# A scan planned in a fixed round of products: one change to a bidirectional RWKV-7 layer on Trainium2

## Chip, cores and metric

The kernel runs on one core of one Trainium2 chip. The metric is the device time of one execution in microseconds (us). Lower is better. The core has a matrix engine (TensorE, PE in the profile; its weight loads are PEld), a vector engine (VectorE, DVE), an activation engine (ScalarE, ACT), a general engine (GpSimd, POOL), a queue engine that issues transfers (SyncE, SP) and 16 DMA engines.

## The reference

One layer over 128 context tokens and 2048 latent tokens of width 1024. Tokens are normalised and modulated, one projection gives eight parts, half of the width goes through a bidirectional RWKV-7 scan (8 heads of 64), the other half through a gated short convolution, and a second projection with a residual and a last normalisation makes the output.

```python
h = _rmsnorm(x, lp['norm_g']) * (1.0 + scale) + shift
proj = h @ lp['w_in']
...
def step(S, inp):
    r_t, w_t, k_t, v_t, kk_t, a_t = inp
    s_kk = jnp.einsum('bdhij,bdhj->bdhi', S, kk_t)
    S = (S * w_t[..., None, :] - s_kk[..., :, None] * (kk_t * a_t)[..., None, :]
         + v_t[..., :, None] * k_t[..., None, :])
    return S, jnp.einsum('bdhij,bdhj->bdhi', S, r_t)
...
yb = b_gate * _short_conv(c_gate * u_conv, lp['conv_w'], is_latent) * jax.nn.silu(g_b)
u = jnp.concatenate([ya, yb], axis=-1) @ lp['w_out']
return x + gate * u, s_final
```

All inputs and outputs are float32.

## The kernel before

The work has three phases. **Phase 1** (`phase1`, from L56) goes over three pairs of token blocks and makes all projections. For each pair, `turn(h, ga, gb)` does a half of group `ga` of the scan's inputs (`mixA`, `gateA`) and, beside it, a half of group `gb` of the convolution (`partB`: `convB` or `gateB`). In the last pair, two convolution groups run in the turns and groups 2 and 3 behind them, in a loop that advances `K.early()`: this generator issues the products F and G of the scan's stages 0 and 1, and their inverses.

**Phase 2** (`phase2`, from L780) is the scan in chunks of 64 tokens. There are 17 stages: 4 head pairs x 4 token blocks of 512, and one for the context. A stage has eight chunks in each direction. For each stage:

- `matrices(s)` (L1078): the products F and G on PE from `rr` (L935), masked from PSUM to SBUF by DVE (L938). The blocks on the diagonal of G are put together by ACT and DVE into `dg` (L947, L950), stored, and loaded as `ab` (`load_ab`).
- `inverse(s)`: `invert` on POOL, L963 to L979, 54 instructions that invert these blocks into `zt`, and a store of `zt` on POOL's own queue. The plan has it as one operation of 24.5 us.
- `blocks(s)` (L1107): loads `zt` back as `zc`, transposes it on DVE to `zr` (L1112), and makes U (L997) and W (L1002) on PE, with copies by ACT.
- `operands` and `merge`: loads, queries Q (transposes, L1022), product X (L1009), and the eight operator products E (L1017), which DVE masks into `E` (L1165).
- `steps(s, i)`: the step of each direction, on PE (L1185). It reads `sv`, and DVE scales its sum by the decay into the next `sv` (L1206): this chain goes through all stages.
- `finish`: normalises outputs and transposes them on PE (T, L1265), gates them (L1269, L1279) and stores them in `mixT`.

Between these, the **filler** (`filler` in `phase3`) multiplies the convolution's half with its half of the output weights: 34 tiles, each of four chunks of three products on PE (L1412 to L1414), a product with the gate (L1418) and a residual addition (L1419) on DVE, and a store.

All of phase 2 is recorded as operations with an engine, a duration and tiles read and written (`Plan.add`). `Plan.order` then builds a schedule by those durations: each time it takes the operation that can start first, and among those the one with the earliest due time; for PE a change of array shape (`mode`) adds `TURN` to the due time and `SWITCH` to the start. The engines then execute their lists in this order, and each engine's list is strict. `LA = 3` stages of F and G are held. `PERIOD = 28000` ns is the distance of due times from stage to stage. PSUM's eight banks are split: two for F, G and Q (`m`), two for other products (`s`), three for steps (`S`) and one for the filler (`f`).

**Phase 3** (`tail`, `rest`): for each of 17 tiles of 128 tokens the scan's half of the output projection (L1365 to L1367), gate, residual, norm, store. Four of these tiles (`EARLY`) are issued before the scan's PSUM banks are given up.

Of the kernel before, what the change touches and what calls it, by code (L numbers as in the profile page):

```python
# [49 lines left out]
def phase1(K):  # L50
# [520 lines left out]
    for t3, js in enumerate(THIRD):  # L571
# [15 lines left out]
        def turn(h, ga, gb):  # L587
# [23 lines left out]
            if first:  # L611
# [14 lines left out]
        for g in range(4):  # L626
            turn(0, g, (g, 0) if t3 < 2 else (g // 2, g % 2))
            turn(1, g, (g, 1) if t3 < 2 else None)
        run(more)
        if t3 == 2:  # L630
# [3 lines left out]
            for g in (2, 3):  # L634
# [46 lines left out]
NST = 17  # L681
LA = 3
PERIOD = 28000
EARLY = 4
SWITCH = 95
TURN = 1200
HOP = 50
# [3 lines left out]
class Plan:  # L691
# [6 lines left out]
    def add(self, eng, fn, ns, r=(), w=(), lag=0, mode=None, alloc=None, use=None, due=1e12):  # L698
        o = Ctx()
        o.eng, o.fn, o.ns, o.lag, o.mode, o.alloc, o.due = eng, fn, ns, lag, mode, alloc, due  # L700
        o.n, o.deps, o.succ, o.users, o.end, o.bank = len(self.ops), set(), [], [], None, []
# [18 lines left out]
    def order(self):  # L720
# [9 lines left out]
        free, mode, done = {}, None, []  # L730
        while any(cand.values()):
            best = None
            for e, l in cand.items():
                at = []
                for o in l:
# [10 lines left out]
                t0 = min(t for t, _ in at)  # L746
                o = min((o for t, o in at if t <= t0), key=lambda o: (o.due + (TURN if e == "PE" and o.mode != mode else 0), o.n))
                if best is None or t0 < best[0]:
                    best = t0, o
            t, o = best  # L750
            cand[o.eng].remove(o)
            if o.eng == "PE":
                t += SWITCH if o.mode != mode else 0
                mode = o.mode
            o.start, o.end = t, t + o.ns + o.lag
# [21 lines left out]
def phase2(K):  # L777
# [7 lines left out]
    def setup_first():  # L785
# [7 lines left out]
        B.mkg = O.r0.tile([128, 2, 128], F32, name="mkg")  # L793
        for i, j in enumerate((0, 2, 4, 5)):
            D(B.msk[:, i], A["msk"][:, j, 0:128])
        for i, j in enumerate((1, 3)):
            D(B.mkg[:, i], A["msk"][:, j, 64:192])
# [14 lines left out]
        B.ztmp = O.rI.tile([128, 512], F32, name="ztmp")  # L812
        B.dgp = O.rI.tile([128, 16], F32, name="dgp")
        B.dg = O.rI.tile([128, 8, 32], F32, name="dg")
# [5 lines left out]
    def setup_rest():  # L820
# [4 lines left out]
        B.banks = dict(m=B.pm, s=bank("s", 2), S=bank("S", 3), f=bank("f", 1))  # L825
# [8 lines left out]
        V.memset(B.geps[:], 64e-5)  # L834
        B.pc = cp.tile([64, 2, 8, 34], F32, name="pc")
# [8 lines left out]
        B.held, B.so = [[cp.tile([64, 2, 64], F32, name=f"{n}{d}") for d in range(2)] for n in ("held", "so")]  # L844
# [92 lines left out]
    def masked(dst, bank, m, mask):  # L937
        V.tensor_tensor(dst[:, m * 4:m * 4 + 4, :], four(bank), mask.unsqueeze(1).broadcast_to((128, 4, 128)), ALU.mult)  # L938
# [7 lines left out]
    def diag_a(s, d):  # L946
        P.activation(B.dg[:], slot(s, d)[1][:, :, 64:96], AF.Identity, scale=B.hm[:, 0:1])  # L947

    def diag_b(s, d):
        V.scalar_tensor_tensor(B.dg[:], slot(s, d)[1][:, :, 96:128], B.hm[:, 1:2], B.dg[:], ALU.mult, ALU.add)  # L950

    def diag_store(s, d):
        nc.scalar.dma_start(S["at"][s][d * 8:d * 8 + 8].rearrange("u s b j i -> (s b j) u i"), B.dg[:])

    def load_ab(s, h):
        D(B.ab[s % 2][h * 64:h * 64 + 64].rearrange("p j i -> p (j i)"), S["at"][s].rearrange("u s b j i -> (u s b) (j i)"))

    def invert(s):
# [3 lines left out]
        tmp, dg = B.ztmp, B.dgp  # L962
        G.memset(zt[:], 0.0)  # L963
        for h in range(2):
            G.memset(zf[h * 64:(h + 1) * 64, h:512:34], 1.0)

        G.tensor_copy(dg[:], ab[:].rearrange("p j i -> p (j i)")[:, 1:1024:66])
        G.tensor_scalar(zf[0:64, 1:512:34], dg[0:64], -1.0, None, ALU.mult)
        tv = tmp[:].rearrange("p (j m) -> p j m", m=16)
        G.tensor_tensor(tv, ab[:, :, 0:32:2], dg[:].unsqueeze(1).broadcast_to((128, 32, 16)), ALU.mult)  # L970
        G.tensor_tensor(ab[:, :, 1:32:2], ab[:, :, 1:32:2], tv, ALU.subtract)
        for m in range(15):
# [6 lines left out]
        G.dma_start(S["zt"][s].rearrange("h u s b q i -> (h u s b) (q i)"), zf)  # L979
# [48 lines left out]
    def early():  # L1028
        setup_first()
        center_states()  # L1030
        for s in range(2):
            for d, units, blk in stages[s]:
# [8 lines left out]
                for m in range(2):  # L1041
                    masked(GA, B.pm[m], m, B.mkg[:, MG[d]])
                diag_a(s, d)
                diag_b(s, d)
                diag_store(s, d)
                yield
            for h in range(2):
                load_ab(s, h)
            invert(s)

    def main():
# [10 lines left out]
        O.lf.close()  # L1062
# [9 lines left out]
    def record(plan):  # L1072
        add = plan.add
        fill = K.filler(O, plan)
        ynew, count = {}, [0]
        pair = lambda f: (lambda *b: f(b))

        def matrices(s):  # L1078

            for d, units, blk in stages[s]:  # L1080
# [4 lines left out]
                for nm, f, dst, mask in (("F", product_F, F, B.msk[:, MF[d]]), ("GA", product_G, GA, B.mkg[:, MG[d]])):  # L1085
                    o = add("PE", lambda *b, f=f, d=d: f(s, d, b), 900, r=rr, mode=QUARTERS, alloc=("m", 2), lag=70)
                    for m in range(2):
                        add("DVE", lambda *b, dst=dst, m=m, mask=mask: masked(dst, b[m], m, mask), 610, w=[(nm, s % LA, d, m)], use=o, lag=70)
                        after(o, plan.ops[-1])
                ga = [("GA", s % LA, d, m) for m in range(2)]  # L1090
                add("ACT", lambda d=d: diag_a(s, d), 330, r=ga, w=[("dg",)], lag=60)
                add("DVE", lambda d=d: diag_b(s, d), 400, r=ga, w=[("dg",)], lag=80)
                add("ACT", lambda d=d: diag_store(s, d), 80, r=[("dg",)], w=[("at", s, d)], lag=3600)
# [447 lines left out]
```

## Time and profile before

| what | us |
|---|---|
| time, median of 3 runs (lowest to highest) | 1781.2 (1778.4 to 1787.8) |
| time of the profiled execution | 1780.8 |
| its span, first to last instruction | 1778.7 |
| first step of the scan starts at | 1033.1 |
| last step of the scan starts at | 1659.9 |

The profile is a page of one execution with views behind it: busy time cut into stretches, instructions in order of time, groups by source line, and waits, each with the instruction or transfer that ended it. An engine's busy share is an average; a matmul's end is modelled, so distances between starts are the safer measure on PE. In a row of instructions the first number is the start, the second the length, and a bracket gives the engine's idle time before it with what ended it.

### The profile page before, as it was taken

To read this page: it belongs to the slowest core of one execution; us is meant where nothing else is said; L and a number is where in the kernel's file an instruction comes from. 1 tells how busy PE (TensorE), PEld (TensorE's weight loads), DVE (VectorE), ACT (ScalarE), POOL (GpSimd) and SP (SyncE) were. 2 spreads that over 40 slices of the span, in tenths; PEclk is the share of its full clock that TensorE was granted. 3 is DMA by queue.
4 is the path that set the end of the run, shared out by engine and by line. 5 is a ranking of instruction groups with operands and counts; after the bars stand their busy time and mean duration, and the time that the engine had idled before them with its cause. 6 is when DMAs were issued, how large, how long until landed. Compare 5 with 4: busy or idle time off the path is not lost. (4 is left out here: it accounts for less than half of the span.)

```text
span 1778.7 us, 40744 instructions
## 1 busy us (share of the span) xinstructions
PE 1586.1 (89%) x16208; PEld 1416.5 (80%) x16208; DVE 1142.3 (64%) x2183; ACT 769.2 (43%) x1568; POOL 602.0 (34%) x1083
## 2 busy tenths in 40 slices
PE   5999899998999998999999668889888997998897
PEld 2889889898999998989998656667766776776685
DVE  5865788866466856547765435676565576565666
ACT  4533455424144433333440245546454553665233
POOL 0011111101011111011120738675775856861153
PEclk8899999999999999999999889999987898998899
DMA  9797788685456655567668388778788789765665
GB/s 361 206 231 215 230 251 256 221 248 144 166 147 208 175 151 158 171 210 216 191 212 295 77 215 218 196 211 241 212 237 215 205 211 248 215 151 171 197 219 183
DMA packets 343070, 368.42 MB, mean 207 GB/s; under 512 B 171160, under 2 KB 276760, under 8 KB 328800
## 3 DMA queue, kind: packets, MB, share of 16 engines
q1 hardware_dynamic: 270576, 356.77, 67.8%
q10 hardware_dynamic: 70944, 4.60, 2.8%
q0 software_dynamic: 1360, 4.46, 0.7%
q8 instruction: 127, 2.08, 0.5%
q14 instruction: 63, 0.52, 0.1%
HBM read 244.75 MB, written 121.00 MB: 206 GB/s over the span
## 5 line engine op out<-in xcount | busy, mean ns | idle before, releaser
L978 POOL TENSOR_TENSOR zt<-zt,ztmp 128x30 f32<-128x30 f32 (+7 forms) x510 | 212.8, 417 | 39.9
L1017 PE MATMUL pss<-str,stl 128*64 128x128 f32 x2176 | 145.3, 283 | 15.0 <-ACT str L1159 10.5
L975 POOL TENSOR_TENSOR ztmp<-ab,zt 128x60 f32<-128x60 f32 (+7 forms) x255 | 139.3, 546 | 19.8
L1017 PEld LDWEIGHTS pss<-str,stl 128*64 128x64 f32 x2176 | 123.3, 142 | 26.4 <-ACT str L1159 15.6
L1185 PEld LDWEIGHTS psS<-sv,E 128*64 128x64 f32 x2176 | 84.8, 143 | 55.7 <-DVE sv L1206 20.9
L1185 PE MATMUL psS<-sv,E 128*64 128x64 f32 x2176 | 105.8, 235 | 21.5 <-DVE sv L1206 12.4
L323 POOL TENSOR_TENSOR shk<-rawl 128x384 f32<-128x384 f32 (+1 forms) x24 | 21.7, 905 | 290.8 <-ACT rawl L319 290.8
L1165 DVE TENSOR_TENSOR E<-pss,msk 128x512 f32<-128x512 f32 x136 | 91.4, 681 | 22.7 <-PE pss L1017 17.6
L935 PE MATMUL psm<-rr 64*64 64x128 f32 x2176 | 84.8, 295 | 20.0 <-DMA rr<-scr_ops 8.8
L935 PEld LDWEIGHTS psm<-rr 64*64 64x64 f32 x2176 | 67.2, 145 | 36.0 <-issue 18.2
L1206 DVE TENSOR_TENSOR sv<-psS,pc 64x128 f32<-64x128 f32 x254 | 64.9, 275 | 33.5 <-PE psS L1185 31.4
L1477 POOL TENSOR_TENSOR z<-z,x 128x512 f32<-128x512 f32 x32 | 48.2, 1512 | 109.1 <-DVE z L1476 94.8
L197 POOL TENSOR_TENSOR hslb<-kd,hshb 128x384 fp32r<-128x384 f32 (+1 forms) x24 | 28.1, 1172 | 167.1 <-ACT hshb L196 159.5
L160 PE MATMUL mmc<-h,w 128*128 128x384 f32 (+1 forms) x192 | 69.4, 361 | 15.4 <-ACT q1r L321 11.8
L1412 PE MATMUL psf<-fwh,fm 128*128 128x512 f32 x136 | 71.6, 526 | 12.1 <-ACT fm L1383 12.1
L323 POOL TENSOR_TENSOR shv<-rawl 128x384 f32<-128x384 f32 (+1 forms) x24 | 21.4, 891 | 157.7 <-ACT rawl L319 132.9
L161 PE MATMUL mmc<-h,w 128*128 128x384 f32 (+1 forms) x192 | 67.4, 351 | 0.0
L162 PE MATMUL mmc<-h,w 128*128 128x384 f32 (+1 forms) x192 | 67.3, 351 | 0.0
L938 DVE TENSOR_TENSOR GA<-psm,mkg 128x512 f32<-128x512 f32 x68 | 44.2, 681 | 35.0 <-PE psm L935 34.9
L938 DVE TENSOR_TENSOR F<-psm,msk 128x512 f32<-128x512 f32 x68 | 44.5, 682 | 33.8 <-PE psm L935 33.7
L160 PE MATMUL mmgb<-h,w 128*128 128x384 f32 (+1 forms) x192 | 64.4, 335 | 0.0
L161 PE MATMUL mmgb<-h,w 128*128 128x384 f32 (+1 forms) x192 | 64.2, 334 | 0.0
(302 smaller groups left out, 5090.9 us busy)
## 6 DMA issues: line engine op xcount, KB each, us to landing
w<-scr_wsp SPq DMA_DIRECT2D x68, 1024.0 KB, 7.2
scr_wsp<-w SPq DMA_DIRECT2D x34, 1024.0 KB, 6.2
rr<-scr_ops SPq DMA_DIRECT2D x64, 512.0 KB, 5.9
scr_ops<-sp SPq DMA_DIRECT2D x160, 192.0 KB, 5.5
wr<-in_win SPq DMA_DIRECT2D x34, 512.0 KB, 6.0
ab<-scr_at SPq DMA_DIRECT2D x34, 256.0 KB, 4.6
fraw<-scr_mixT SPq DMA_DIRECT2D x34, 256.0 KB, 4.7
fx<-in_x SPq DMA_DIRECT2D x34, 256.0 KB, 5.1
```

What stands on the lines that cost most here:

```text
L160: T.matmul(ps[:, :n], w[:, 0, k], hh[:, 0, k, :n], start=k == 0, stop=False)
L161: T.matmul(ps[:, :n], w[:, 0, k], hh[:, 1, k, :n], start=False, stop=False)
L162: T.matmul(ps[:, :n], w[:, 1, k], hh[:, 0, k, :n], start=False, stop=k == 7)
L935: T.matmul(four(banks[m])[rows64(place(u, hd)), i, :].rearrange("p (a b) -> p a b", b=64), w[r, u, :], x[r, :, u, :], start=True, stop=True)
L938: V.tensor_tensor(dst[:, m * 4:m * 4 + 4, :], four(bank), mask.unsqueeze(1).broadcast_to((128, 4, 128)), ALU.mult)
L975: G.tensor_tensor(tv, ab[:, j:j + 2, j + 2:32].unsqueeze(1).broadcast_to((128, kn, 2, n)), zt[:, :kn, j:j + 2].unsqueeze(3).broadcast_to(( ...
L978: G.tensor_tensor(zt[:, :kn, j + 2:32], zt[:, :kn, j + 2:32], tv[:, :, r], ALU.subtract)
L1017: T.matmul(pe[c, i, hd, :].rearrange("p (b t) -> p b t", b=2), B.lt[d][:, x, hd, u], B.rt[d][:, :, hd, u], start=True, stop=True)
L1165: after(o, add("DVE", lambda b, d=d, k=k: V.tensor_tensor(B.E[d][n][:, k:k + 2].rearrange("p a b c -> p (a b) c"), b[:].rearrange("p (a c) ...
L1185: T.matmul(sums(b)[x, q, hd, :], B.E[d][n][:, k, hd, x], sv[:, u, hd, :], start=True, stop=True)
L1206: after(o, add("DVE", lambda b, dst=dst, q=q, d=d, p=p, c=c: V.tensor_tensor(dst, sums(b)[0:64, q], B.pc[0:64, d, 2 * p:2 * p + 2, c:c + 1 ...
L1412: T.matmul(b[:], ms[0][:, k], w[0][:, k], start=k == 0, stop=False)
```

## The change

The planner gets a fixed round for PE. Every PE operation now carries a place `at = (round, name)`, and PE takes operations in that order, looking at most `WINDOW` operations ahead.

```diff
-EARLY = 4
-SWITCH = 95
-TURN = 1200
-HOP = 50
+SWITCH = 100
+HOP = 60
+WINDOW = 6
+LATE = 150
+ROUND = ["S0", "E10", "S1", "E11", "S2", "E12", "S3", "E13", "U*", "W*", "X0*", "S4", "E00", "S5", "E01", "S6", "E02", "S7", "E03",
+         "Q", "T0", "G0", "f0", "f1", "G1", "X1", "U", "F0", "T1", "W", "f2", "X0", "F1", "f3"]
...
+                for o in turn[:-WINDOW - 1:-1] if e == "PE" else l:
...
+                if e == "PE":
+                    t0, o = min(at, key=lambda x: (x[0] + (SWITCH if x[1].mode != mode else 0) + LATE * (len(turn) - 1 - turn.index(x[1])), x[1].n))
+                else:
+                    t0 = min(t for t, _ in at)
+                    o = min((o for t, o in at if t <= t0), key=lambda o: (o.due, o.n))
```

The places: F and G of stage s in round s - 4, U and W in round s - 2 (of stage 1 in round 0, at the starred places), X and Q of the first half in round s - 2 and of the second in s - 1, the first four E in round s - 1, the other four and the steps in round s, T in s + 1, and two filler tiles in every round from -1 to 15 (`f0` to `f3`, half a tile each). Durations in the plan are new throughout, for example 281 in place of 236 ns for a step.

```diff
-            add("POOL", lambda: invert(s), 24500, r=[("ab", s % 2, 0), ("ab", s % 2, 1)], w=[("ztd", s)], lag=3900)
+            add("ACT", lambda: cleared(s), 620, w=[("zt", s % 2)], lag=60)
+            ab = [("ab", s % 2, 0), ("ab", s % 2, 1)]
+            add("POOL", lambda: invert(s), 3500, r=ab, w=[("zt", s % 2)])
+            for i, ms in enumerate((range(0, 4), range(4, 7), range(7, 11), range(11, 15))):
+                add("POOL", lambda ms=ms: eliminate(s, ms), 5300, r=ab, w=[("zt", s % 2)], lag=70 if i == 3 else 0)
+            add("SP", lambda: store_inverse(s, nc.sync), 400, r=[("zt", s % 2)], w=[("ztd", s)], lag=3000)
...
-            add("DVE", lambda: V.tensor_tensor(z[:], z[:], x[:], ALU.add), 600, r=[("fx",)], w=[("fz",)], lag=70)
+            add("POOL", lambda: G.tensor_tensor(z[:], z[:], x[:], ALU.add), 1370, r=[("fx",)], w=[("fz",)], lag=70, due=due + 2000)
```

`cleared` writes zeros into `zt` on ACT; before, a memset on POOL did it. `eliminate` is the loop that stood at the end of `invert`; `invert` now reads its diagonal from `ab` directly (no copy to `dgp`) and works in two halves with a scratch tile of half the size. `store_inverse` is the store of `zt`, now on SP's queue. In the scan the filler's residual addition is on POOL.

Fewer copies: the diagonal of G is no longer put together. G's right half, which needs no mask, goes from PSUM to SBUF by an ACT copy and its left half by DVE, and four stores on ACT's queue take the diagonal blocks straight from there.

```diff
     def diag_store(s, d):
-        nc.scalar.dma_start(S["at"][s][d * 8:d * 8 + 8].rearrange("u s b j i -> (s b j) u i"), B.dg[:])
+        for sl in range(2):
+            for b in range(2):
+                r = slice(sl * 64 + b * 32, sl * 64 + b * 32 + 32)
+                nc.scalar.dma_start(S["at"][s][d * 8:d * 8 + 8, sl, b].rearrange("u j i -> j u i"), slot(s, d)[1][r, :, 64 + b * 32:96 + b * 32])
```

E of the first half of a stage is split in the same way between ACT and DVE. Two full-height ACT operations in place of four copies of 32 rows place `zc` in `zb`. The squares in `finish` go to a PSUM bank, which ACT allocates. PSUM is split into five banks for all products but the steps (`s`) and three for steps (`S`).

In phase 1, one more convolution group stands behind the first F and G:

```diff
-            turn(0, g, (g, 0) if t3 < 2 else (g // 2, g % 2))
+            turn(0, g, (g, 0) if t3 < 2 else {1: (0, 0), 3: (0, 1)}.get(g))
...
-            for g in (2, 3):
+            for g in (1, 2, 3):
```

At the end, four output tiles of phase 3 are recorded in the plan (`project`, new), in place of the four early ones; `tail` leaves them out and then has all eight PSUM banks.

```diff
+    PLANNED = [(9, 16, "Q"), (10, 17, "S0"), (11, 17, "G0"), (12, 17, "U")]
+
+    def project(O2, plan, after):
...
+                o = add("PE", mm, 2800, r=[("amh", j), ("aml", j)] + [("wo", k, n, a) for k in range(4) for a in range(2)], mode=FULL, alloc=("s", 1), lag=70, at=(s, nm))
...
-        for _ in range(1 + EARLY):
-            next(tail)
+        next(tail)
         O.p2.close()
+        O.pm.close()
...
-        for i in TILES:
+        for i in [i for i in TILES if i not in [x[0] for x in PLANNED]]:
```

More of the change, by code (lines that the diff above doesn't have):

```diff
@@ L1216, in outputs @@
             if y is None:
[L1217 to L1218 removed]
+                y = spare.pop(0)
                 ynew[p, blk] = y, there
@@ L1295, in record @@
             merge(s, 1)
-            for i in range(4):
-                steps(s, i)
+            if s + LA < NST:
+                matrices(s + LA)
             if s + 1 < NST:
```

325 lines of the change are left out of this document (202 added, 123 removed).

## The prediction

> **What bounds the kernel now.** I read the page first, then busy time cut into stretches, then PE's and POOL's instructions in order of time, then who waited for whom.
>
> ```profile
> PE 1586.1 (89%) x16208; PEld 1416.5 (80%) x16208; DVE 1142.3 (64%) x2183; ACT 769.2 (43%) x1568; POOL 602.0 (34%) x1083
> ```
>
> TensorE (PE) looks like the bound, but 89% is an average over three parts. The stretches separate the gap before the scan, the scan, and the projection behind it; the last row holds eleven whole stages of the scan.
>
> ```profile
> 1003.00:1033.00 30.00, 10.54 (x201) 8.53 (x200) 9.90 (x17) 14.23 (x30) 26.24 (x56) 0.66 0.57 150
> 1033.00:1660.00 627.00, 539.13 (x9935) 430.42 (x9936) 390.62 (x793) 329.31 (x658) 388.26 (x817) 0.91 0.78 207
> 1660.00:1778.70 118.70, 100.48 (x424) 79.40 (x424) 77.09 (x118) 40.72 (x107) 48.17 (x32) 0.92 0.64 210
> ```
>
> ```profile
> 1125.10:1544.70 419.60, 369.56 (x6766) 292.51 (x6762) 271.51 (x541) 222.57 (x447) 285.73 (x591) 0.90 0.84 224
> ```
>
> The columns are length, busy time of PE, PEld, DVE, ACT and POOL, granted clock, DMA share, GB/s. A stage takes 419.6/11 = 38.1 us; in it DVE works 24.7 and ACT 20.2, so neither bounds. What must PE spend? I take the distance from one start to the next, which does not rest on modelled ends:
>
> ```profile
> 1217.94 0.66 PE L1265 MATMUL pss<-idt,y 128*128 128x128 f32 x4
> 1218.44 0.38 PE L1022 MATMUL psm<-idt,be 128*128 128x128 f32 x2
> 1218.75 0.45 PE L1185 MATMUL psS<-sv,E 128*64 128x64 f32 x8
> 1219.13 1.20 PE L1002 MATMUL pss<-zc,zr 32*32 32x32 f32 x64
> 1220.26 0.45 PE L1185 MATMUL psS<-sv,E 128*64 128x64 f32 x8
> 1220.64 1.10 PE L935 MATMUL psm<-rr 64*64 64x128 f32 x32
> 1221.68 0.50 PE L1412 MATMUL psf<-fwh,fm 128*128 128x512 f32 x1
> ...
> 1222.57 1.10 PE L1009 MATMUL pss<-F,zb 64*64 64x128 f32 x32
> ...
> 1227.12 1.97 PE L1017 MATMUL pss<-str,stl 128*64 128x128 f32 x32
> 1229.01 0.45 PE L1185 MATMUL psS<-sv,E 128*64 128x64 f32 x8
> ...
> 1245.81 0.40 PE L1185 MATMUL psS<-sv,E 128*64 128x64 f32 x8
> 1246.04 1.05 PE L1017 MATMUL pss<-str,stl 128*64 128x128 f32 x16
> 1246.91 0.40 PE L1185 MATMUL psS<-sv,E 128*64 128x64 f32 x8
> ```
>
> Between changes of array shape: transposes T 0.50, queries Q 0.31, a step 0.38, W (and U, as many matmuls) 1.13, F or G 1.04 (X, of the same shape, too), a filler chunk 0.89, an operator product E 1.89/2 = 0.945. A stage has 1 T, 4 Q, 16 steps, U and W, 4 F/G, 2 X, 8 chunks and 8 E: 0.50 + 1.24 + 6.08 + 2.26 + 4.16 + 2.08 + 7.12 + 7.56 = 31.0 us. So 7 of the 38.1 us are waits and reduced clock. Now POOL, which inverts one set of blocks a stage:
>
> ```profile
> 1471.94 0.20 POOL L967 COPY dgp<-ab 128x16 f32<-128x16 f32 x1 [0.38 <-DMA ab<-scr_at]
> 1472.24 0.27 POOL L968 TENSOR_SCALAR zt<-dgp 64x16 f32<-64x16 f32 x1
> ...
> 1500.49 0.62 POOL L979 DMA_DIRECT2D scr_zt<-zt  x1 [0.30 <-POOL zt L978]
> ```
>
> ```profile
> POOL dgp L967 <- DMA ab<-scr_at: 88.5, 10, 18.2
> ```
>
> One inverse lasts 1500.49 + 0.62 - 1471.94 = 29.2 us, and in those eleven stages POOL waited 88.5 us, 8.0 a stage, for `ab`, the blocks that G makes. 29.2 + 8.0 is nearly the stage. **The scan runs at a loop's pace**: G on PE comes late, the inverse starts late, and everything that needs it comes late. G, U and X stand where the due times put them.
>
> **The change, part by part.** *The round.* Each F and G now stands at (s-4), U at (s-2), about two rounds apart. Two rounds of 30 us cover `ab`'s way plus a 29 us inverse, so I let the 8.0 us go. What is late next is POOL itself. Per inverse the change removes the copy into dgp (1472.24 - 1471.94 = 0.30) and the store's issue with its wait (0.30 + 0.62); the clearing of zt goes to ACT, and was outside the 29.2; the ones' memsets, in its shadow until now, fall inside (0.3, an estimate from the 0.27 of the scaling of 64 rows); two 512-wide operations become four halves, two more starts (0.2, an estimate). 29.2 - 0.9 - 0.3 + 0.3 + 0.2 = 28.5 us. The filler's additions arrive on POOL, two a stage:
>
> ```profile
> L1477 POOL TENSOR_TENSOR z<-z,x x32: 1278/1303/2267, 1673.7 to 1766.2; 128x512 f32<-128x512 f32 x32
> ```
>
> That row (shortest, median, longest, ns) is the same operation in the tail: between 1.3 and 2.3; I take 1.5, near the median with the start between two, because DVE is equally busy in the scan. POOL then needs 28.5 + 2 x 1.5 = 31.5 us a round, against 27.4 us in the planner's new entries (3.5 + 4 x 5.3 + 2 x 1.37). POOL falls behind its plan and becomes the pace.
>
> *PE in the round.* Steps and operator products form one run of equal shape: a step then costs 1246.04 - 1245.81 = 0.23 and E 0.87. 16 x 0.15 + 8 x 0.075 = 3.0 us less: PE needs 28.0 us, under POOL's 31.5. So these 3.0 us buy slack rather than time. Where E covers a step, the next step's wait for its decay on DVE is hidden; in the second half of the last stage no E is left, and PE waits.
>
> *Copies, masks, banks.* The half masks and the lost diagonal copy lower DVE; ACT gets half the copies and zt's clearing. At 24.7 and 20.2 us a stage both stay below 31.5: nothing, so long as they do. The five shared PSUM banks make a late eviction block the next allocation in order; I give that no term of its own but put it with the waits below. `cleared` makes ACT wait for the store two stages back, and behind it stand the copies that feed E; POOL's previous inverse, 28 us, is the cover.
>
> *Queues.* The inverse's store leaves POOL's queue for SP's. SP then waits for the inverse's end, with the loads of the next stage behind it. SP already waited at the next instruction, the load of zc, so I price the move at zero, and its failure as a rival. The four diagonal stores in place of one move the same bytes. The DMA share, 0.84 over 38.1 us, would be 32.0 us of full share at today's packet times: a second thing near 31.5, and a reason not to forecast the floor.
>
> *Start.* One conv group (two halves) moves from the turns behind the first F and G, so these and the first inverse come earlier, PE's sum staying the same.
>
> ```profile
> 966.30 1.12 PE L935 MATMUL psm<-rr 64*64 64x128 f32 x32
> ...
> 1002.82 0.28 PE L162 MATMUL mmb<-h,w 128*128 128x256 f32 x1
> 1018.91 1.92 PE L997 MATMUL pss<-zr,GA 32*32 32x32 f32 x64 [15.81 <-DVE zr L1112]
> ```
>
> ```profile
> 983.64 0.21 POOL L967 COPY dgp<-ab 128x16 f32<-128x16 f32 x1 [49.29 <-DMA ab<-scr_at]
> ...
> 1068.22 0.20 POOL L967 COPY dgp<-ab 128x16 f32<-128x16 f32 x1 [28.10 <-DMA ab<-scr_at]
> ...
> 1608.92 0.60 POOL L979 DMA_DIRECT2D scr_zt<-zt  x1 [0.30 <-POOL zt L978]
> ```
>
> From G to the inverse it takes 983.64 - 966.30 = 17.3 us. PE sat idle 15.81 us for the first inverse; that gap fills. F and G of stage 2, whose inverse now starts at 1068.22 after POOL waited 28.1 us, stand at the front of the new order, directly behind phase 1: G at about 1007, the inverse at 1007 + 17.3 = 1024, 44 us earlier. The first steps start no earlier (about 1031 against 1033), since two filler tiles and F/G of stages 2 and 3 now precede them.
>
> *End.*
>
> ```profile
> 1659.89 0.45 PE L1185 MATMUL psS<-sv,E 128*64 128x64 f32 x8 [0.31 <-DVE sv L1206]
> ```
>
> From the last inverse to the last step it is 1659.89 - 1608.92 = 51.0 us, from there to the end of the span 118.8. The four planned output tiles do not shrink PE's work; they fill idle time around the last steps: I take 5 us off the 118.8, between 0 and the 16 us that PE's busy 100.5 of 118.7 leaves.
>
> **The sum** goes along POOL, with R for the mean round of the fifteen inverses left at 1024: 1024 + 15 R + 51.0 + 113.8 + 2.1, the last because the profiled execution took 1780.8 us around its span of 1778.7 us; that is 0.4 us under the median of 1781.2. So **1191 + 15 R**. Today R = (1608.92 - 1068.22)/15 = 36.05. The floor R = 31.5 gives 1663. I do not take the floor: PE with 28.0 us at today's granted 0.90 needs 31.1, DMA 32.0, POOL 31.5, and three queues in order that run level make each other wait. Of the 4.5 us between 31.5 and 36.05 I leave 1.7: R = 33.2, **1689 us**, 5.2% less.
>
> **Rivals.**
> 1. *POOL shortens too.* The fastest inverse of the trace:
>
> ```profile
> 1098.19 0.21 POOL L967 COPY dgp<-ab 128x16 f32<-128x16 f32 x1
> ...
> 1124.94 0.61 POOL L979 DMA_DIRECT2D scr_zt<-zt  x1 [0.30 <-POOL zt L978]
> ```
>
> It took 27.4 us with its issue, 26.7 after the edits; with two additions at 1.3 R = 29.3 to 31.5: 1631 to 1663. For: DVE loses work. Against: PE and DMA would then bind.
>
> 2. *Waits move and do not go.* The plan counts 27.4 us for POOL where 31.5 are due, so PE meets U late, idles, and its clock falls (0.66 in the gap before the scan). R from 34.3 to 38.7; unchanged at 36.05 it is 1191 + 541 = 1732, and only the earlier start and the tail remain. The Trainium skill, "TensorE: Matmul & The Clock Gate", "Why this matters for your kernels", warns against idle gaps over about 3 us, since the clock then halves; by that rule PE's spare 31.5 - 28.0 = 3.5 us, if it lies in one wait, would run the next 7 us of its work at half speed and so cost 3.5 us more, R = 35.0 and 1716 (an estimate). The 0.66 of the gap agrees.
>
> 3. *The addition hurts the inverse.* At 2.27 us each, R = 28.5 + 4.5 = 33.0 before any wait, 1686, and with the 1.7 us of waits 1712. The Trainium skill, "GPSIMD Engine Reference", section 1 "Specifications", says GpSimd shares its SBUF interfaces with VectorE and contends with instructions of two SBUF inputs; the spread 1278 to 2267 ns of one shape agrees, and speaks against moving an addition there.
>
> 4. *Slower: SP blocks the next inverse.* If SP's order has stage s+1's operands for F and G, or its `ab`, behind the store of inverse s, POOL starves for G's way: R up to 31.5 + 17.3 = 48.8, 1923. It decides from R = 39.9 (1790), that is from 8.4 us of such waiting a round. Against: G stands two rounds ahead, so `ab` should have been loaded.
>
> 5. *No change to speak of*: R = 38.7 to 39.9, the same loss eating all of the start.
>
> **How the numbers follow.** A measurement of this kernel tells about 0.5% (1772 to 1790) from no change. Forecast, R 31.5 to 34.3 (1663 to 1706): 0.39. Rival 1: 0.13. Rival 2, 1706 to 1772: 0.26, of it 0.10 for the halved clock. Rival 3, 1686 to 1712: 0.09. Rival 5: 0.05. Rival 4: 0.08. Faster 0.87, same 0.05, slower 0.08. The range 1640 to 1755 cuts the lower third of rival 1 and the upper quarter of rival 2, and all of 4 and 5: about 0.2 left out.
>
> **What would show it.** POOL with no wait for `ab` in mid-scan, inverses 28 to 29 us and starts 31 to 34 us apart; inverse 2 at about 1024; no 15.8 us gap before the first U; E and steps in one run at 0.23 and 0.87; U waiting on zr each round if POOL paces. Wrong if POOL still waits for `ab` (round), if inverses grow past 31 us (port), if PE's longest waits are for operands and not for zr (DMA or SP), or if phase 1 ends later than about 1008 because the turns lost their cover.

## The result and the profile after

| | before | after | forecast |
|---|---|---|---|
| time, median (lowest to highest), us | 1784.4 (1778.4 to 1787.8) | 1808.0 (1804.9 to 1812.3) | 1689 (1640 to 1755) |
| ratio to before, 95% interval | | 1.014 (1.010 to 1.018) | 0.948 |
| span of the profiled execution, us | 1778.7 | 1803.1 | |

The kernel became 1.4% slower. The page of after, busy time by engine:

```profile
PE 1571.4 (87%) x16208; PEld 1427.0 (79%) x16208; DVE 1080.1 (60%) x2116; ACT 788.4 (44%) x1653; POOL 618.7 (34%) x1102
```

No share rose by more than a point, so the page does not say where the time went. Busy time of after, cut into the same stretches as before the change: the gap ahead of the first step, the scan, what is behind it, and the eleven stages 2 to 12 (length, busy PE, PEld, DVE, ACT, POOL, granted clock, DMA share, GB/s):

```profile
1007.40:1070.20 62.80, 34.34 (x548) 26.87 (x548) 21.95 (x42) 26.66 (x60) 31.41 (x65) 0.73 0.82 216
1070.20:1680.80 610.60, 498.50 (x9597) 423.38 (x9596) 315.46 (x708) 335.48 (x712) 380.57 (x783) 0.88 0.76 203
1680.80:1803.10 122.30, 100.46 (x413) 79.13 (x412) 73.42 (x114) 38.73 (x103) 46.40 (x32) 0.90 0.56 187
1148.20:1581.70 433.50, 347.04 (x6739) 295.99 (x6738) 222.00 (x489) 233.27 (x501) 294.57 (x601) 0.87 0.78 207
```

The last row is the one to read. In these eleven stages TensorE's work fell from 369.6 to 347.0 us, but the stretch grew from 419.6 to 433.5: TensorE's idle time went from 50.0 to 86.5 us, at a granted clock of 0.87 where it was 0.90. The round did what it was made for, as TensorE's instructions in order of time show (start, length):

```profile
1306.89 1.05 PE L1039 MATMUL psm<-str,stl 128*64 128x128 f32 x16
1307.77 0.40 PE L1222 MATMUL psS<-sv,E 128*64 128x64 f32 x8
1308.00 1.05 PE L1039 MATMUL pss<-str,stl 128*64 128x128 f32 x16
```

An operator product takes 1307.77 - 1306.89 = 0.88 and a step 0.23, as forecast. The idle time lies in the other half of the round, where F, G, U and W follow each other, and its source stands on ScalarE. One place of after, ScalarE, then VectorE, then TensorE in order of time:

```profile
1321.27 3.63 ACTq L967 DMA_DIRECT2D scr_at<-GA  x4
1324.94 0.37 ACT L1116 COPY GA<-psm 128x256 f32<-128x256 f32 x1 [4.94 <-DMA scr_at<-GA]
```

```profile
1325.34 0.42 DVE L955 TENSOR_TENSOR GA<-psm,mkg 128x256 f32<-128x256 f32 x1 [4.62 <-ACT GA L1116]
```

```profile
1325.82 1.73 PE L1019 MATMUL psm<-zr,GA 32*32 32x32 f32 x64 [4.61 <-DVE GA L955]
1327.48 0.80 PE L1467 MATMUL pss<-fwh,fm 128*128 128x512 f32 x1
```

A group of four stores holds ScalarE's queue for 3.63 us, of which 1.5 us is issuing; what the rest is stands in the last section. The copy of the next G stands behind it, and ScalarE has been idle for 4.94 us when the copy starts. VectorE's half of the same bank waits for that copy, and TensorE waits 4.61 us for VectorE. Then U's 64 matmuls take 1.66 us, from their start to the next product's, where the 64 of W, without a wait ahead, took 1.13 before the change. The granted clock fell: it was 1.00 during the wait, 0.60 over U, and 0.50 from 1326.2 to 1332.9. The Trainium skill, "TensorE: Matmul & The Clock Gate", section "Why this matters for your kernels", says that an idle gap of over about 3 us drops the throughput; this row agrees. So a wait is paid for again in the work behind it.

Who waited on ScalarE for the stores, and for the store of the inverse, between 1114 and 1581 us of after (us in total, times, longest):

```profile
ACT zt L973 <- DMA scr_zt<-zt: 37.4, 9, 8.2
...
ACT zb L1150 <- DMA scr_at<-GA: 19.9, 5, 5.2
...
ACT GA L1116 <- DMA scr_at<-GA: 12.8, 3, 4.9
...
ACT fm L1431 <- DMA scr_at<-GA: 4.1, 1, 4.1
...
ACT stl L1165 <- DMA scr_at<-GA: 2.9, 1, 2.9
```

There are two suspects: the four stores, and the clearing of `zt` (`cleared`, L973), whose waits for the store of an earlier inverse are even the larger number.

### The profile page after: what moved, and what is told of

The parts are those of the page before. It is cut to its first block, busy times and chain, and to the rows that moved or that the text cites. A ratio compares the mean times of both kernels' runs of the same rounds, so it can differ in the third digit from the quotient of the medians.

```text
span 1803.1 us, 40948 instructions
## 1 busy us (share of the span) xinstructions
PE 1571.4 (87%) x16208; PEld 1427.0 (79%) x16208; DVE 1080.1 (60%) x2116; ACT 788.4 (44%) x1653; POOL 618.7 (34%) x1102
## 3 DMA queue, kind: packets, MB, share of 16 engines
q10 hardware_dynamic: 72576, 4.61, 2.9%
## 4 chain that ended last, share of the span: by engine, by line
PE 36%; DMA 28%; DVE 14%; ACT 7%; POOL 7%; issue 6%; SPq 3%; ACTq 1%; DVEq 0%; POOLq 0%
DMA scr_ops<-sp 9%; DMA scr_at<-GA 3%; POOL zt L998 3%; DMA scr_zt<-zt 3%; DMA wr<-in_win 2%; PE psS L1222 2%; POOL ztmp L995 2%; PE pss L1039 1%; DMA out_y<-z 1%; PE mmc L160 1%; DMA scr_vt<-vt 1%; DMA ab<-scr_at 1%; PE mmc L161 1%; DMA sv<-scr_vt 1%; PE mmc L162 1%
## 5 line engine op out<-in xcount | busy, mean ns | idle before, releaser
L998 POOL TENSOR_TENSOR zt<-zt,ztmp 128x30 f32<-128x30 f32 (+7 forms) x510 | 203.9, 400 | 39.9
L1222 PEld LDWEIGHTS psS<-sv,E 128*64 128x64 f32 x2176 | 86.6, 147 | 51.8 <-DVE sv L1244 42.8
L951 PE MATMUL pss<-rr 64*64 64x128 f32 x1216 | 75.1, 307 | 16.5 <-DMA rr<-scr_ops 8.3
L1039 PE MATMUL pss<-str,stl 128*64 128x128 f32 x1216 | 82.8, 280 | 0.5 <-issue 0.4
L951 PEld LDWEIGHTS pss<-rr 64*64 64x64 f32 x1216 | 59.3, 153 | 29.2 <-issue 15.9
L1476 POOL TENSOR_TENSOR fz<-fz,fx 128x512 f32<-128x512 f32 x34 | 44.8, 1319 | 101.1 <-DVE fz L1475 85.4
L951 PE MATMUL psm<-rr 64*64 64x128 f32 x960 | 62.0, 296 | 14.9 <-DVE GA L955 7.5
L1039 PEld LDWEIGHTS pss<-str,stl 128*64 128x64 f32 x1216 | 68.4, 142 | 1.4 <-issue 0.7
L1039 PE MATMUL psm<-str,stl 128*64 128x128 f32 x960 | 66.1, 282 | 3.2 <-ACT stl L1188 2.6
L197 POOL TENSOR_TENSOR hsls<-sq,hshs 128x384 fp32r<-128x384 f32 (+1 forms) x24 | 25.7, 1071 | 122.0 <-ACT hshs L196 103.5
L160 PE MATMUL mmg<-h,w 128*128 128x384 f32 (+1 forms) x192 | 64.5, 336 | 0.0
L160 PE MATMUL mmgb<-h,w 128*128 128x384 f32 (+1 forms) x192 | 64.0, 334 | 0.4 <-ACT q1r L321 0.4
```

Source lines behind the costliest of these rows:

```text
L160: T.matmul(ps[:, :n], w[:, 0, k], hh[:, 0, k, :n], start=k == 0, stop=False)
L197: eng.tensor_tensor(lo[:, :n], t_[:, :n], hi[:, :n].bitcast(F32), ALU.subtract)
L951: T.matmul(four(banks[m])[rows64(place(u, hd)), i, :].rearrange("p (a b) -> p a b", b=64), w[r, u, :], x[r, :, u, :], start=True, stop=True)
L998: G.tensor_tensor(zt[:, :kn, j + 2:32], zt[:, :kn, j + 2:32], tv[:, :, r], ALU.subtract)
L1039: T.matmul(pe[c, i, hd, :].rearrange("p (b t) -> p b t", b=2), B.lt[d][:, x, hd, u], B.rt[d][:, :, hd, u], start=True, stop=True)
L1222: T.matmul(sums(b)[x, q, hd, :], B.E[d][n][:, k, hd, x], sv[:, u, hd, :], start=True, stop=True)
```

## The experiments

Every batch of runs timed the kernel before again, with medians from 1773 to 1784 us, so it is the ratios that are compared. The table has every run. "Stage" is the time from the first step of stage 0 to the first step of stage 13, divided by 13; the next two columns are the starts of the first step and of the first step of stage 1.

| run | ratio to before (95%) | stage, us | first step | stage 1 |
|---|---|---|---|---|
| before | 1 | 39.4 | 1033.1 | 1074.9 |
| after | 1.014 (1.010 to 1.018) | 39.3 | 1070.2 | 1114.6 |
| e1_one_store | 0.987 (0.985 to 0.989) | 35.0 | 1071.8 | 1102.4 |
| e2_pool_clear | 1.013 (1.010 to 1.015) | 39.3 | 1064.9 | 1111.9 |
| e3_priced | 0.994 (0.992 to 0.996) | 36.9 | 1054.4 | 1097.2 |
| e4_late_fill | 1.012 (1.008 to 1.016) | 39.9 | 1044.9 | 1097.5 |
| e6_four_of_dg | 1.001 (0.998 to 1.003) | 37.9 | 1064.7 | 1099.0 |
| e7_one_store_late_fill | 0.990 (0.988 to 0.993) | 36.2 | 1054.7 | 1099.7 |
| e8_stores_on_SP | 0.999 (0.997 to 1.002) | 38.1 | 1054.9 | 1097.2 |
| e9_before_four | 1.006 (1.003 to 1.009) | 39.4 | 1029.5 | 1069.0 |
| e10_counted_410 | 1.018 (1.015 to 1.022) | 39.1 | 1074.8 | 1111.1 |
| e11_add_on_DVE | 0.978 (0.974 to 0.981) | 34.9 | 1071.6 | 1106.5 |
| e12_two_groups | 0.992 (0.989 to 0.995) | 35.6 | 1072.2 | 1103.6 |
| e13_add_and_groups | 0.988 (0.984 to 0.991) | 35.6 | 1081.9 | 1117.2 |
| e14_copies_kept_GA | 0.998 (0.996 to 1.000) | 37.1 | 1072.1 | 1103.4 |
| e15_rr_loaded_early | 0.983 (0.980 to 0.986) | 36.9 | 1048.7 | 1100.5 |

### Four stores or the clearing

One store again, with the two copies that put its tile together:

```diff
+                add("ACT", lambda d=d: diag_a(s, d), 330, r=ga, w=[("dg",)], lag=60)
+                add("DVE", lambda d=d: diag_b(s, d), 400, r=ga, w=[("dg",)], lag=80)
-                add("ACT", lambda d=d: diag_store(s, d), 240, r=ga, w=[("at", s, d)], lag=3600)
+                add("ACT", lambda d=d: diag_store(s, d), 80, r=[("dg",)], w=[("at", s, d)], lag=3600)
```

> The diagonal blocks of GA are again put together in one tile (one ScalarE and one VectorE instruction) and stored by one DMA per direction, in place of four stores on ScalarE's queue; all else is the changed kernel (1808 us). Theory A (the four stores hold ScalarE: a group takes 1.8 to 4.2 us of its queue, about 2.8, where the plan counts 0.24, and what stands behind them, copies that TensorE waits for, is late): two groups a stage and 13 stages with two groups of some 2.5 us too much are 65 us of ScalarE time; if half of it reaches TensorE the stages 0 to 12 fall from 39.35 to about 37 us and the kernel to 1770 to 1790 us. Theory B (the clearing on ScalarE is what holds it): stages at 39 us, 1800 to 1815 us. Theory D (the fixed order itself sets the stage, through the wait of the steps for VectorE and of products for operands): no change, 1800 to 1815 us, and VectorE's 0.4 us more per direction may show as a few us.

The clearing back on GpSimd:

```diff
-            add("ACT", lambda: cleared(s), 620, w=[("zt", s % 2)], lag=60)
...
+        G.memset(zt[:], 0.0)
```

> The tile of the inverse is cleared again on GpSimd, as the first instruction of the inverse, in place of the ScalarE write; all else is the changed kernel (1808 us). Theory B (the clearing waits on ScalarE for the store of the inverse before last: 37.4 us in nine waits between 1114 and 1581 us of the span, 51 us in all): stages 0 to 12 fall by 2 to 3 us each, to 36.5 to 37.5, and the first step comes some 8 us earlier (one wait of 13.6 us stands before it), 1765 to 1785 us. Theory A (the four stores): at most 1 us per stage, 1795 to 1810 us. Theory D (the fixed order): no change.

One store takes the ratio from 1.014 to 0.987, some 47 us of 1781, more than theory A expected; moving the clearing changes nothing that the intervals show. The larger wait was the harmless one, at least beside the four stores; the clearing was not moved without them. Stages 2 to 12 of the run with one store, one of its stores among ScalarE's instructions in order of time, and GpSimd's waits in the eleven stages:

```profile
1137.80:1527.30 389.50, 343.19 (x6898) 291.33 (x6898) 233.58 (x512) 245.13 (x527) 305.61 (x614) 0.90 0.86 230
```

```profile
1305.38 0.37 ACTq L971 DMA_DIRECT2D scr_at<-dg  x1
```

```profile
POOL zt L987 <- DMA ab<-scr_at: 25.7, 6, 8.4
POOL ztmp L990 <- DMA ab<-scr_at: 7.6, 7, 2.0
```

TensorE has nearly the same to do as in after (343.2 against 347.0 us) and is idle for 46.3 us instead of 86.5: of the 44.0 us between the two stretches 40.2 are its idle time. The clock is back at 0.90.

### The hold, the plan, the place

Only the plan's number for a group of stores is changed, from 240 to 2800 ns, then from 240 to 410:

```diff
-                add("ACT", lambda d=d: diag_store(s, d), 240, r=ga, w=[("at", s, d)], lag=3600)
+                add("ACT", lambda d=d: diag_store(s, d), 2800, r=ga, w=[("at", s, d)], lag=3600)
```

> One number of the plan alone is changed: a group of four stores counts 2800 ns of ScalarE time instead of 240, so the order is laid out around what the profile shows; the instructions are the same as in the changed kernel (1808 us). Theory C (the harm of the four stores is that the plan does not know them): at least half of what the run with one store gains, 1780 to 1795 us. Theory A (ScalarE is held whatever the order): less than a third of it, 1800 to 1812 us. Theory D: no change.

> The changed kernel (ratio 1.014) with one number of its plan moved a little: a group of four stores counts 410 ns instead of 240, which is what the copy and the store of the run with four stores of one tile (ratio 1.001) count on ScalarE. Theory C (a plan that counts the group at too little lays the waits where TensorE needs them; 0.17 us more of some 3 corrects almost nothing): 1.010 to 1.016, as the changed kernel. Rival (the order of a plan moves the time by about a per cent whatever is changed in it, so that the step from 1.014 to 1.001 says nothing of the copies): a ratio off by 0.006 or more from 1.014, most likely below.

With the same instructions in another order, 0.994: three quarters of what one store gives comes from the plan knowing the price. The groups are not shorter there: from first issue to last they hold ScalarE for 3.4 us on average, 2.8 in after. It is what stands behind them that changed. 0.17 us more gave nothing; its 1.018 lies a little above what theory C allowed and 0.4% from after, less than the 0.6% of the rival. So this one new order moved the time by less than half a per cent. It is one order only: differences of a per cent and more are taken as real below, smaller ones are not.

Next, the order of the run with one store, with its store split in four, and the same with the stores reading GA while the copies are made all the same:

```diff
-        nc.scalar.dma_start(S["at"][s][d * 8:d * 8 + 8].rearrange("u s b j i -> (s b j) u i"), B.dg[:])
+        for sl in range(2):
+            for b in range(2):
+                r = slice(sl * 64 + b * 32, sl * 64 + b * 32 + 32)
+                nc.scalar.dma_start(S["at"][s][d * 8:d * 8 + 8, sl, b].rearrange("u j i -> j u i"), B.dg[r])
```

> The run with one store (1751 us, ratio 0.987), with the same plan and order, but its one store is split into four on ScalarE's queue: same tile, same bytes, same rows, one issue more by three. Theory A (four issues in a row hold ScalarE for 2 us or more, in whatever order): the hold per group grows from 0.37 us to 2 to 4 us, stages 0 to 12 from 35.0 to 37.5 to 39.5 us, 1780 to 1810 us. Rival (the order that the plan lays out without the copies is what cost, not the hold): 1745 to 1760 us, stages within 0.7 us of 35.0.

> The run with four stores of the copied tile (ratio 1.001) with the four stores reading GA itself: the copies are still made, in the same order, and only the source of the stores differs; the changed kernel (1.014) has the same stores without the copies. Theory of place (the copies put the stores one VectorE instruction later in ScalarE's queue, where less waits behind them): 0.998 to 1.006. Theory of source (stores out of GA are slower to issue or to land than out of a tile with the blocks side by side): 1.010 to 1.020, with holds of a group longer than the 3.3 us on average of the run with the copied tile.

Splitting one store, nothing else, costs 0.987 to 1.001, 24 us. Reading GA instead of the tile costs nothing more (0.998, with 3.2 us a group). So after is 1.6% slower than a kernel that does all its work and two more copies for each group. The copies put the stores behind an instruction of VectorE, so that something else stands behind them. Who waited on ScalarE for the stores in that run, in the window shown for after:

```profile
ACT pss L1306 <- DMA scr_at<-GA: 19.1, 2, 12.2
...
ACT stl L1199 <- DMA scr_at<-GA: 8.3, 1, 8.3
...
ACT zb L1161 <- DMA scr_at<-GA: 7.3, 2, 4.9
...
ACT stl L1176 <- DMA scr_at<-GA: 6.5, 1, 6.5
...
ACT str L1176 <- DMA scr_at<-GA: 3.2, 1, 3.2
```

The sum, 44.4 us, is no smaller than the 39.7 of after. But 19.1 of it is met by the square of a finished output (L1306), which feeds no product of the coming stages, and 25.3 by operands of their products (`stl`, `zb`, `str`). In after it is 35.6 of 39.7 (`zb`, GA, `stl`). How much of the 1.6% is this and how much is other changes of the order that come with the copies was not told apart.

The stores on SyncE's queue, and the kernel before with the four stores alone:

```diff
-                add("ACT", lambda d=d: diag_store(s, d), 240, r=ga, w=[("at", s, d)], lag=3600)
+                add("SP", lambda d=d: diag_store(s, d, nc.sync), 1600, r=ga, w=[("at", s, d)], lag=3600)
```

> The four stores of each group, without the copies, issued from SyncE in the scan, with 1.6 us of its queue in the plan; all else is the changed kernel (1808 us). Theory A (it is ScalarE's queue that is held): the stages fall as with one store or better, to 34 to 36 us, 1740 to 1760 us. Rival (the store itself is the trouble, its issue on any queue, or its late landing for the inverse): SyncE then holds the loads behind it, stages 37 us and more, 1775 to 1810 us.

> The kernel before with this one part of the change: the two copies that put the diagonal blocks together and their one store become four stores straight from GA on ScalarE's queue, counted 240 ns in the plan. Theory A: the hold of ScalarE appears here too, about 2.5 us a group, and the stages 0 to 12 grow from 39.35 us by 1 to 4 us: 1785 to 1820 us. Rival (the hold does harm only where the order of TensorE is fixed): within 8 us of before, faster or slower, since the list of the kernel before goes round a late operand.

On SyncE the stores gain 1.4% against after, but no more than the rival said. Another wait grew: the store of the inverse stands on the same queue, and the clearing on ScalarE waits for it (between 1114 and 1581 us; 37.4 in after):

```profile
ACT zt L973 <- DMA scr_zt<-zt: 71.2, 8, 14.6
```

That this wait is what eats the gain is not shown; in after the same wait did no harm.

In the kernel before, the four stores, with the copies gone, cost 0.6%, 10 us of 1777, a little over the 8 that the rival allowed and a fifth of what they cost in after. The groups hold ScalarE as long there, 3.1 us on average. Its stages 0 to 12 do not grow; from the first step of stage 13 to the last step it takes 131.1 us instead of 115.2, which neither theory said. I read from it that a list by due times finds its way round a held engine in mid-scan better than a fixed round; no run shows that alone.

### What sets the pace once the stores are gone

The filler's addition back on VectorE, on top of one store:

```diff
-            add("POOL", lambda: G.tensor_tensor(z[:], z[:], x[:], ALU.add), 1370, r=[("fx",)], w=[("fz",)], lag=70, due=due + 2000)
+            add("DVE", lambda: V.tensor_tensor(z[:], z[:], x[:], ALU.add), 680, r=[("fx",)], w=[("fz",)], lag=70, due=due + 2000)
```

> The run with one store (ratio 0.987, 35.0 us a stage, an inverse every 33.8 us between stages 2 and 13) with the filler's addition back on VectorE, 0.68 us in the plan. Theory P (with ScalarE free GpSimd's inverse and its additions set the pace, as the prediction had it: two additions of 1.5 us go from each period): inverses every 30 to 32 us, stages 0 to 12 at 32 to 33.5 us, ratio 0.970 to 0.979. Rival (TensorE, busy 88% of that stretch at a granted clock of 0.91, sets the pace and GpSimd only nearly): inverses as far apart as the stages, 34 to 35.5 us, ratio 0.983 to 0.992.

This is the fastest version, 0.978, faster than both kernels. The ratio lies in theory P's range, but by luck: a stage takes 34.9 us against 35.0, inverses start 34.0 us apart with the addition on either engine, and 4.3 of the 7.7 us between the two spans lie behind the last step (120.9 us against 125.2), for a reason that no run shows. GpSimd's waits for `ab` in the eleven stages say why the pace stays:

```profile
POOL zt L987 <- DMA ab<-scr_at: 49.9, 8, 11.2
POOL ztmp L990 <- DMA ab<-scr_at: 8.9, 8, 1.9
```

Against the run with one store they grew from 33.3 to 58.8 us, 2.3 a stage, about what two additions of 1.32 us took (L1476, mean of after). GpSimd waits for as much as it no longer works; something else is the pace. TensorE is the fullest engine, busy for 343.2 of 389.5 us with one store. But with the addition on VectorE it is busy for 330.2 of 386.1, at a granted clock of 0.94 instead of 0.90, and the stage is no shorter; so its work alone is not the pace either. The DMA share, 0.86 in both, is a rival that no run tested. What sets the pace stays open.

### The start

The filler pieces of the round before the first step moved to the round of stage 13, in after and with one store:

```diff
-        slots = [(-1, f"f{i}") for i in range(4)]
+        slots = []
...
-            slots += [(s, f"f{i}") for i in range(4)]
+            slots += [(s, f"f{i}") for i in range(4)] * (2 if s == NST - 4 else 1)
```

> The four filler pieces that the changed kernel places in the round before the first step are done in the round of stage 13, beside its own four; all else is the changed kernel (1808 us, first step at 1070 us). Theory S (the first step is late because two filler tiles and their operands stand ahead of it in the fixed order): PE's own 9.5 us of them and the wait of 6.8 us for their operand go, the first step comes at 1054 to 1062 us; the end comes 8 to 16 us earlier less what round 13 takes back (at most 4), 1793 to 1804 us. Rival (the first step is late because the operands of stage 2's matrices are loaded behind the last stores of phase 1, which moves everything): first step within 4 us of 1070, 1803 to 1812 us.

> The run with one store (1751 us, first step at 1072 us) and the four filler pieces of the round before the first step done in the round of stage 13. Theory S (the fillers ahead of the first step are part of the late start, hidden in the run with four stores by what held ScalarE): first step at 1045 to 1058 us and 1735 to 1745 us. Rival (what the start gains is given back in stage 0, whose operands come no sooner): the first step earlier, the second step's stage at the same time as before, 1747 to 1755 us.

Two conv groups behind the first F and G instead of three, with one store and with the addition on VectorE as well:

```diff
-            turn(0, g, (g, 0) if t3 < 2 else {1: (0, 0), 3: (0, 1)}.get(g))
+            turn(0, g, (g, 0) if t3 < 2 else (g // 2, g % 2))
```

> The run with one store (ratio 0.987) with two conv groups behind the first F and G, as before the change, instead of three: the first F comes some 17 us later, at about 955 us, and inverse 0 ends near 1010. Theory S2 (the early start of F, G and inverse 0 is worth nothing, since U of stage 0 stands 40 us behind the end of inverse 0 in the run with one store): the first step within 6 us of 1072 us, ratio 0.983 to 0.990. Rival (the third group is what starts the chain early, as the prediction had it): the second stage's inverse and steps come later by 10 us or more, ratio 0.992 to 1.000.

> Both of these together on the run with one store: the addition on VectorE and two conv groups. If the two act apart, the ratio is 0.987 plus what each changes; theory P with S2 gives 0.970 to 0.980, the rivals 0.985 to 1.000.

The operands of stage 2's F and G loaded in phase 1, in the kernel with one store and the addition on VectorE:

```diff
+            if s == 1:
+                for d, units, blk in stages[2]:
+                    for part in range(2):
+                        load_rr(d, units, blk, part)
```

> The run with one store and the addition on VectorE (ratio 0.978), with the operands of stage 2's F and G loaded in phase 1, behind F and G of stage 1, instead of with the scan's first loads, which stand in SyncE's queue behind the last stores of phase 1. Theory S3 (the first step is late because F and G of stage 2 wait for these loads: 7.4 us of wait on TensorE, and 22.6 us of SyncE's queue held by a store of phase 1): the wait for rr goes, inverse 2 starts 8 to 14 us earlier than 1062, the first step 6 to 14 us earlier than 1072, ratio 0.969 to 0.975. Rival (TensorE's stretch up to the second step is full anyway and the time is not gained, as with the fillers moved): the second step within 4 us of 1106 and the ratio 0.975 to 0.982.

That these loads are late shows in after's waits from 985 (SyncE's queue) and 1005 us to 1072:

```profile
SPq L526 <- DVE bsv L521: 23.0, 1, 23.0
```

```profile
PE pss L951 <- DMA rr<-scr_ops: 8.3, 2, 7.4
```

The first step can be had 17 to 25 us earlier in three ways, and none pays. With one store stage 1 starts at 1099.7 instead of 1102.4 (e7) and at 1100.5 instead of 1106.5 (e15), and the ratios are no better than without the edit (0.990 against 0.987, 0.983 against 0.978; in e7 the crowded stage 13 takes 37.9 us instead of 24.0). In after, stage 1 does start 17 us earlier (e4), and the ratio, 1.012 against 1.014, stays within the intervals. The steps of the last of these runs (count, shortest/median/longest ns, first and last start):

```profile
L1234 PE MATMUL psS<-sv,E x8: 222/222/270, 1048.7 to 1049.0; 128*64 128x64 f32 x8
```

```profile
L1234 PE MATMUL psS<-sv,E x14: 222/222/270, 1100.5 to 1100.9; 128*64 128x64 f32 x14
```

Between them lie 51.8 us, against 34.9 without the edit: of the 22.9 us that the first step gains, stage 0 gives back 16.9, and by the first step of stage 13 the run is 3 us behind. The ratio missed theory S3, and the second step came 6 us earlier, where the rival allowed 4. The third conv group is worth 0.4% with one store, where the intervals touch, and 1.0% with the addition on VectorE: the first step does not show it in the one pair (1072.2 against 1071.8) and shows 10 us in the other. The two edits together give 0.988 where their sum would be 0.982: they do not act apart.

## Why the prediction was wrong

Its sum was: inverse 2 starts at 1024, then 15 R, then 51.0 to the last step, then 113.8. The same points in after, and in the run with one store (instructions in order of time):

```profile
1045.10 0.28 POOL L983 TENSOR_SCALAR zt<-ab 64x16 f32<-64x16 f32 x1 [24.33 <-DMA ab<-scr_at]
...
1607.61 0.60 POOL L998 TENSOR_TENSOR zt<-zt,ztmp 128x30 f32<-128x30 f32 x2
```

```profile
1680.85 0.56 PE L1222 MATMUL psS<-sv,E 128*64 128x64 f32 x8
```

```profile
1057.17 0.28 POOL L987 TENSOR_SCALAR zt<-ab 64x16 f32<-64x16 f32 x1 [32.76 <-DMA ab<-scr_at]
...
1575.09 0.60 POOL L1002 TENSOR_TENSOR zt<-zt,ztmp 128x30 f32<-128x30 f32 x2
```

| term, us | forecast | after | one store |
|---|---|---|---|
| inverse 2 starts | 1024 | 1045.1 | 1057.2 |
| R, of fifteen | 33.2 | 37.5 | 34.6 |
| last inverse to last step | 51.0 | 72.6 | 48.1 |
| last step to end | 113.8 | 122.3 | 125.2 |
| span | 1686.8 | 1803.1 | 1749.0 |

- **The step that failed**, and turned the sign, is one sentence: "The four diagonal stores in place of one move the same bytes", priced at zero. It counted bytes; the price is paid in issues, in their waits for earlier transfers to land, and in what stands behind them on ScalarE. It cost 2.7% of the time, some 47 of the 119 us between forecast and result, and most of two terms: R and the way from the last inverse to the last step are 4.3 and 21.6 us over the forecast in after, 1.4 over and 2.9 under with one store. The rest of the miss stays with one store: 62 us over the forecast span, 33 from the start of inverse 2, 21 from fifteen R and 11 behind the last step, less those 2.9. The same step let ScalarE pass because it was busy for 20.2 us a stage. Busy time does not count the issue of a DMA: the engine's share stood at 44% while its queue was held.
- *The clearing* was priced at zero, rightly (e2), but for a wrong reason. The previous inverse does not cover it: it waits up to 8.2 us in the scan and 13.6 us once before the first step. That nothing which TensorE needed stood behind it for long enough is my reading.
- *GpSimd as the pace* was wrong. With ScalarE free R is 34.6, near 33.2, but taking GpSimd's additions away leaves the stage at 34.9 (e11). The waits for `ab`, on which the loop's pace was argued, are slack that takes up what GpSimd has left. TensorE's busy time came down by 22.5 us in eleven stages, 2.0 a stage of the 3.0 forecast, and by 2.4 with one store, at the same granted clock as before (0.90). What the round alone does to the time no run shows.
- *The start* failed twice. Inverse 2 came 21 us later than said: its last G came at 1030.7, not at about 1007, since the products of stage 2 waited 8.3 us for operands whose loads stand in SyncE's queue behind stores of phase 1, 4.9 us for ScalarE, and stood behind one another. e15 takes the wait for the loads away, its inverse 2 eliminates 17 us earlier (from 1047.4 instead of 1064.8), and nothing is gained: inverse 2 does not set the time. And the 37 us by which the first step is later than before are partly work done ahead (F and G of stage 4 now come before the first step of stage 1, where they came 31 us behind it) that is missing at the end: from the first step of stage 13 to the last step it is 99.2 us against 115.2.
- *The end*: 5 us less were forecast, 3.5 more came, 6.4 more with one store. The third stretch has nearly all of TensorE's work still in it, 100.46 us busy of 122.30 as against 100.48 of 118.70. No run tried this alone.
- *Of the rivals*, the second, waits that move and do not go, has the right shape and holds the measured R (34.3 to 38.7), though not the time (at most 1772); its place was wrong. It put the fault in the plan's time for GpSimd. The fault was in the plan's time for ScalarE, 240 ns for a group that takes 3.63 us in the row shown. The rival that ended slower, SyncE blocking the next inverse, did not happen: GpSimd's waits for `ab` fell from 88.5 to 55.6 us in eleven stages. The contention of the addition is not seen either: its mean is 1.32 us.

## What to carry to other kernels

Price a DMA that a computing engine issues as an instruction of that engine, once for each issue. Ask what each issue has to wait for, and look at what stands behind it on that queue; the engine's busy share does not show it. Where lists are planned ahead, a wrong duration of one small operation can cost more than the operation: correcting the number alone gave back 2%. And a first step, or a wait, that moves is no gain until the next fixed point moves too: follow it to the next stage before counting it.

## What was not expected of the hardware

Four DMAs issued in a row take longer than four times one. Stores of after on ScalarE's queue between 1100 and 1600 us (count, shortest/median/longest ns, first and last start):

```profile
L967 ACTq DMA_DIRECT2D scr_at<-GA x100: 309/369/2017, 1102.4 to 1568.9; - x100
```

```profile
DMA to landing us min/median/max: 1.7/3.7/7.5
```

These are 25 groups, from first issue to last 1.8 to 4.2 us, 69.9 in all, of which 24.9 lie between the issues. No view of the profile names what ended these gaps, but the trace holds, for each instruction, the semaphores (counters that engines wait on) that it waits for. The transfers of ScalarE and SyncE count their landings on the same eight semaphores, used in turn, 173 or 174 transfers on each in after. Before its issue, nearly every store (128 of 136) waits until the earlier transfer on its semaphore has landed.

33 of the gaps, 23.3 of the 24.9 us, end 0.02 us behind such a landing. In the group shown above, loads landed at 1322.73 and 1324.03, and stores were issued at 1322.75 and 1324.05. With the same wait ahead of a group's first store, the 25 groups take 77.8 us of ScalarE: 45.0 us of issuing and 32.8 us in 44 such waits, 43 of them for a transfer that SyncE had issued. With one store it is 9.4 and 12.6 us. On SyncE's own queue (e8), 24 groups wait 2.0 us in all. These waits are written into the program and are no limit of the engine; no run took them away alone.

The Trainium skill, "DMA: Bandwidth & Descriptors", section "Issuing engines are not separate DMA queues", says that the time to initiate a DMA is usually small relative to the DMA itself. For one issue (0.37 us against a landing after 3.7) the trace agrees. A group of four holds the engine for 2.8 us on average, and 1.8 of these are issuing.
